# Turning attention probabilities on VectorE and through DRAM, in a streaming encoder layer

## The chip, the cores and the metric

One core of one Trainium2 chip runs the program. The metric is the time of one execution on the device in microseconds. TensorE (PE) multiplies matrices and writes PSUM; VectorE (DVE) and ScalarE (ACT) do the element-wise work; GpSimd (POOL) only clears memory at the start. SyncE (SP) issues the loads of weights; ACT issues all other transfers except part of the first loads and last stores. All numbers are float32. A product in near float32 accuracy is made of `fp32r` operands: a value is split into a high part (a rounded copy) and a low part (the rest), and high x high, high x low and low x high are added up.

## The reference

One layer on 256 prompt tokens and 64 sample tokens, 320 together, model width 2048:

```
xn = rmsnorm(x)
h  = xn @ w_in                      # columns [u | v | q | k | v_attn]
u, v = gelu(h[u]), gelu(h[v])       # gMLP branch, 2048 wide each
q, k = rope(h[q]), rope(h[k])       # 32 query heads, 4 key heads, 64 wide
a  = u * (masked ws @ layernorm(v) + bs)      # mixing inside chunks of 128 tokens
s  = q k^T / 8, by chunks of 64 queries       # keys: this chunk and the two before it
p  = exp(s - m) / (sum exp(s - m) + exp(sink - m))
o  = p @ v_attn
x += (sigmoid(g_a) * (a @ w_branch_a) + sigmoid(g_b) * (o @ w_branch_b)) @ w_out
x += swiglu(rmsnorm(x));  y = rmsnorm(x)
```

The outputs are y for both token sets, the new keys and values, and the normalised v of the sample.

## The kernel before

Activations stay in SBUF with features on partitions and the 320 tokens along the row, split into a high and a low part (`xh`, `xl`). Weights are streamed. `gemm` (line 136) makes 512 output columns: for each block of 256 contraction rows it takes a weight block, already split into `hi` and `lo`, and issues 24 matmuls with 320 columns. `fetch` (119) loads raw blocks of 512 KB on SP, four buffers deep; `prepare` (128) splits a block two blocks ahead, `hi` on ACT (L107) and `lo` on DVE (L110), three buffers deep. If either is late, PE waits. The order of products is in `products` (49): first k and v_attn (`kv`), then the four q and four v products in the order of `QV`, then the gate of the attention branch (`mm_gb`), its branch product (`mm_bb`), u, the other gate, the other branch, w_out and the feed-forward part.

All other work is put between the matmuls by a calendar. `later(slots, fn)` (90) books a function some slots ahead; `pump` (96) runs after every twelve matmuls and issues what is due. So a `gemm` of 16 contraction chunks has 16 slots. After the `kv` product the framework may also reorder instructions when it schedules.

The attention works on a group of 8 query heads with one key head at a time (`g` of 4). `q_done` (515) copies a q product out of PSUM, swaps the rope halves with four small transfers issued by ACT (`rope_swap`, 329), turns them on DVE (`rope_turn`), splits the queries into high and low (`q_parts`, 421), and books five steps, five slots apart, beginning `QK0[g]` slots after the product. A step `n` takes 64 queries of 8 heads as 4 tiles of 128 rows, against 64, 128 or 192 keys (`NK`); its keys' values are in one or two blocks of 64 or 128 keys (`VB`). It has four functions (`attend`, 441):

- `scores`, slot 0: 8 matmuls into two PSUM banks; maximum on DVE; exponential on ACT, which also adds up the denominator, into `pr`.
- `weigh`, slot 2: multiplies `pr` by the reciprocal denominator, two tiles on ACT and two on DVE.
- `turn`, slot 4: turns `pr` by TensorE, four transposes per key block into the PSUM tile `pt` (L486), and splits it into `ph` and `pl` (both called `p` for a block of 64 keys, whose other 64 partitions are zero).
- `values`, slot 6: for each key block two matmuls, value block `vv` with `ph` and with `pl` (L501). A value block holds the high parts in columns 0 to 63 and the low parts in 64 to 127, so partitions 0 to 63 of the result `o` are from the high values and 64 to 127 from the low ones. ACT copies the lower half out (L503), DVE adds both into `f1` (L509).

The blocks of new values are made by `new_v` (395): two transposes of v_attn per block (L398), a scale by the rms factor (`rv`, one column per block), a split. Five blocks are made; two groups of tokens are transposed twice, as blocks start at tokens 0, 64, 128, 192 and 256.

`v_done` (538) takes a v product: scale, gelu, transposes back to tokens (L547), statistics. Behind the attention come, from the calendar, the split of `f1` (`split_o`, 578) and the layer norm of v (`v_load` 589, `v_norm` 596).

Of the kernel before, what the change touches and what calls it, by code (L numbers as in the profile page):

```python
# [18 lines left out]
P = 128  # L19
# [14 lines left out]
    [(0, 4), (512, 4), (1024, 4), (1536, 4)],  # L34
    [(0, 4), (512, 4), (1024, 4), (1536, 2), (1792, 2)],
]
QV = [("q", 0), ("v", 0), ("q", 1), ("q", 2), ("v", 1), ("q", 3), ("v", 2), ("v", 3)]
QK0 = [14, 14, 24, 18]

NK = [64, 128, 192, 192, 192]  # L40
KC = [0, 0, 0, 64, 256]
VB = [[(0, 64)], [(0, 128)], [(0, 128), (2, 64)], [(1, 128), (3, 64)], [(4, 128), (5, 64)]]


def f32(ap):
    return ap.bitcast(F32)
# [23 lines left out]
def tile_hybrid_step(ctx: ExitStack, tc: tile.TileContext, a: dict, outs: list):  # L70
# [158 lines left out]
    rv = main.tile([P, 6], F32, name="rv")  # L229

    def x_norm():
        ssum = main.tile([P, 3], F32, name="ssum")
# [14 lines left out]
    def put_rope():  # L247
        nc.vector.tensor_tensor(cos_t, cos_t, rx, op=ALU.mult)
        nc.vector.tensor_tensor(sin_t, sin_t, rx, op=ALU.mult)
        for blk, i, p0, q0, n in (  # L250
            (0, 0, 0, 0, P), (1, 0, 64, 0, 64), (1, 1, 0, 64, 64), (2, 1, 0, 0, P), (3, 1, 64, 0, 64), (5, 2, 0, 0, 64)
        ):
            nc.vector.tensor_copy(rv[q0 : q0 + n, blk : blk + 1], rs1[p0 : p0 + n, i : i + 1])

    xt_d = dram.tile([P, DC, T], F32, name="xt_d")
    xst = {}
# [85 lines left out]

    ka = ap.tile([P, 4, NPOS], F32R, name="ka")
    kl = ap.tile([P, 4, NPOS], F32R, name="kl")
    vv = ap.tile([P, 6, 4, P], F32R, name="vv")
    vat = qr[:, 2:4, :]
    p64 = ap.tile([P, 2, 512], F32R, name="p64")
    nc.gpsimd.memset(f32(p64[64:P]), 0.0)
    for blk in (3, 5):
        nc.gpsimd.memset(f32(vv[64:P, blk]), 0.0)  # L350
    ck = ap.tile([P, 2, P], F32, name="ck")

    def split_v(blk, n, src):
        split(vv[:n, blk, :, 0:64], vv[:n, blk, :, 64:128], src.rearrange("p (g d) -> p g d", g=4))

    def rope_scale():
        nc.vector.tensor_scalar_mul(cos_t, cos_t, 0.125)
# [30 lines left out]
    def cached():  # L388
        pc = bank("pc")
        for t in range(2):  # L390
            nc.tensor.transpose(pc[:, t * P : (t + 1) * P], ckv[:, 0, t * P : (t + 1) * P], ident)
        nc.vector.tensor_copy(ck, pc[:, 0:256].rearrange("p (t k) -> p t k", t=2))
        split_v(4, P, ckv[:, 1, :])

    def new_v(blk, t0, n):
        pv = bank(f"pv_{blk}")
        for t in range(2):
            nc.tensor.transpose(pv[:n, t * P : (t + 1) * P], vat[:, t, t0 : t0 + n], ident)  # L398
        v = tmp.tile([P, 256], F32, tag="e1", name=f"vn_{blk}", bufs=4)[:n]
        nc.vector.tensor_scalar_mul(v, pv[:n, 0:256], rv[:n, blk : blk + 1])  # L400
        split_v(blk, n, v)
        if blk in (2, 5):
            dst = vo_p if blk == 2 else vo_s
# [37 lines left out]
    def attend(g, n, qs, st):  # L441
        nk, kc = NK[n], KC[n]

        def scores():
            sp = [bank(f"s_{g}_{n}_{i}") for i in range(2)]
            mx = ap.tile([P, 4], F32, tag="mx", name=f"mx_{g}_{n}", bufs=2)
            for j in range(4):
                o = sp[j // 2][:, (j % 2) * 256 : (j % 2) * 256 + nk]
                q2 = qs[:, j * 5 + n, :, :].rearrange("p e q -> p (e q)")
                nc.tensor.matmul(o, q2, ka[:, g, kc : kc + nk], start=True, stop=False)  # L450
                nc.tensor.matmul(o, q2, kl[:, g, kc : kc + nk], start=False, stop=True)
            for i in range(2):
                v = sp[i].rearrange("p (j k) -> p j k", j=2)[:, :, 0:nk]
                nc.vector.reduce_max(mx[:, 2 * i : 2 * i + 2], v, axis=AX.X)
            nm = ap.tile([P, 4], F32, tag="nm", name=f"nm_{g}_{n}", bufs=2)
            nc.vector.scalar_tensor_tensor(nm, mx, -1.0, nsink[:, 4 * g : 4 * g + 4], ALU.mult, ALU.min)
            es = ap.tile([P, 4], F32, tag="es", name=f"es_{g}_{n}", bufs=2)
            nc.vector.tensor_tensor(es, sink[:, 4 * g : 4 * g + 4], nm, op=ALU.add)
            nc.scalar.activation(es, es, AF.Exp)
            pr = ap.tile([P, 4, 192], F32, tag="pr", name=f"pr_{g}_{n}", bufs=2)  # L460
            den = ap.tile([P, 4], F32, tag="den", name=f"den_{g}_{n}", bufs=2)
            for j in range(4):
                o = sp[j // 2][:, (j % 2) * 256 : (j % 2) * 256 + nk]
                nc.scalar.activation(
                    pr[:, j, 0:nk], o, AF.Exp, bias=nm[:, j : j + 1], accum_out=den[:, j : j + 1]
                )
            st.update(pr=pr, den=den, es=es)

        def weigh():
            den, pr = st["den"], st["pr"]  # L470
            nc.vector.tensor_tensor(den, den, st["es"], op=ALU.add)
            nc.vector.reciprocal(den, den)
            for j in range(4):
                p = pr[:, j, 0:nk]
                if j % 2:
                    nc.vector.tensor_scalar_mul(p, p, den[:, j : j + 1])
                else:
                    nc.scalar.activation(p, p, AF.Copy, scale=den[:, j : j + 1])

        def turn():  # L480
            k0 = 0
            mm = []
            for bi, (blk, kn) in enumerate(VB[n]):
                pt = bank(f"pt_{g}_{n}_{bi}")
                for j in range(4):
                    nc.tensor.transpose(pt[:kn, j * P : (j + 1) * P], st["pr"][:, j, k0 : k0 + kn], ident)  # L486
                k0 += kn
                if kn == P:
                    ph = ap.tile([P, 512], F32R, tag="ph", name=f"ph_{g}_{n}")
                    pl = ap.tile([P, 512], F32R, tag="pl", name=f"pl_{g}_{n}")  # L490
                else:
                    ph, pl = p64[:, 0, :], p64[:, 1, :]
                split(ph[:kn], pl[:kn], pt[:kn])
                mm += [(vv[:, blk, g, :], ph), (vv[:, blk, g, :], pl)]
            st["mm"] = mm

        def values():
            po = bank(f"o_{g}_{n}")
            mm = st["mm"]
            for i, (l, r) in enumerate(mm):  # L500
                nc.tensor.matmul(po, l, r, start=(i == 0), stop=(i == len(mm) - 1))  # L501
            ol = tmp.tile([64, 512], F32, tag="st", name=f"ol_{g}_{n}")
            nc.scalar.activation(ol, po[64:128], AF.Copy)  # L503
            pov = po.rearrange("p (j e q) -> p j e q", j=4, e=2)
            olv = ol.rearrange("p (j e q) -> p j e q", j=4, e=2)
            oc = slice(4 * g, 4 * g + 4)
            tq = slice(n * 64, (n + 1) * 64)
            for e in range(2):
                nc.vector.tensor_tensor(  # L509
                    f1[64 * e : 64 * e + 64, oc, tq], pov[0:64, :, e, :], olv[:, :, e, :], op=ALU.add  # L510
                )

        return scores, weigh, turn, values

    def q_done(g, ps):
        for t in range(4):
            nc.scalar.activation(qr[:, t, :], ps[t], AF.Copy)
        qs = ap.tile([P, 20, 2, 64], F32R, tag="qs", name=f"qs_{g}")
        hi, lo = q_parts(g, qs)
        later(1, lambda: rope_swap(4))  # L520
        later(5, lambda: rope_turn(0))
        later(7, lambda: rope_turn(2))
        at = QK0[g]
        later(at - 5, lambda: hi(0))
        later(at - 4, lambda: lo(0))
        later(at - 3, lambda: hi(1))
        later(at - 2, lambda: lo(1))
        for n in range(5):
            scores, weigh, turn, values = attend(g, n, qs, {})
            later(at + 5 * n, scores)  # L530
            later(at + 5 * n + 2, weigh)
            later(at + 5 * n + 4, turn)
            later(at + 5 * n + 6, values)


    bst = main.tile([P, 3, 4, 6], F32, name="bst")
# [82 lines left out]
    at = 16  # L619
# [8 lines left out]
    later(at + 46, lambda: nc.scalar.dma_start(gv_s[0, 0], tok[0:64, 2, :]))  # L628
    later(at + 39, load_ws)
    later(at + 42, lambda: turn_ws(0))  # L630
    later(at + 43, lambda: turn_ws(1))

    def sigmoid(dst, ps, b0, g):
        for t in range(4):
# [247 lines left out]
```

## Time and profile before

| | |
|---|---|
| median of 3 runs | 1971.21 us (1970.22 to 1971.97) |
| the profiled execution | 1970.76 us |
| its span in the trace | 1968.9 us |
| PE / DVE / ACT busy | 99% / 52% / 42% of the span |
| first `mm_q` to first `mm_gb` | from 47 to 322 us |
| first scores, last values | 103 us, 353 us |

Busy time of PE counts overlapping matmuls once; their ends are modelled, so a busy PE says only that it was not waiting. Instructions that issue a transfer are not counted as busy; they show in rows marked ACTq and SPq. In rows of groups the columns are line, engine, operation, output and inputs, shapes and count, then busy time, the mean of one in ns, and the idle time in front of them with what ended it. In rows of the chain and of the timeline they are start, duration, what. A row of waits gives who waited for whom, the sum, how often, the longest. A row of windows gives the stretch and its length, then each engine's busy time and number of instructions, the clock granted to TensorE, the share of the DMA engines, and GB/s.

### The profile page before, as it was taken

The numbers are of one execution on the slowest core, as the hardware profiler recorded it, in microseconds if no ns is written. First come the engines' busy times: TensorE is split into PE (matmuls) and PEld (weight loads), VectorE is DVE, ScalarE is ACT, GpSimd is POOL, SyncE is SP. The second block draws the span as 40 slices with busy tenths as digits, with TensorE's granted clock in tenths as the row PEclk, the third lists the DMA queues.
The fourth block names the chain that finished last, engine by engine and source line by source line (L and its number), as shares of the span: only waits on it lengthen the run. The fifth ranks groups of instructions, "written<-read, shape, count | busy, mean of one in ns | idle before, by whom it ended". The sixth has DMA issues, their size and how long they took to land.

```text
span 1968.9 us, 31812 instructions
## 1 busy us (share of the span) xinstructions
PE 1948.7 (99%) x13327; PEld 1940.0 (99%) x13327; DVE 1028.6 (52%) x1513; ACT 817.1 (42%) x1219; POOL 5.6 (0%) x11
## 2 busy tenths in 40 slices
PE   9999999999999999999999999999999999999997
PEld 8999999999999999999999999999999999999996
DVE  5767777853445543454455444443444444444454
ACT  5575766633333443333343333333333333333343
POOL 1000000000000000000000000000000000000000
PEclk9999999999999999999999999999999999999998
DMA  8544433654444454445455555445555544555433
GB/s 266 157 121 133 118 112 118 181 184 150 150 140 139 140 150 150 150 150 204 150 150 149 147 152 151 150 147 151 149 149 148 153 151 149 147 151 150 152 130 102
DMA packets 152304, 294.82 MB, mean 150 GB/s; under 512 B 9521, under 2 KB 14593, under 8 KB 151969
## 3 DMA queue, kind: packets, MB, share of 16 engines
q1 hardware_dynamic: 147104, 281.05, 46.8%
q10 hardware_dynamic: 5056, 11.74, 1.9%
q8 instruction: 104, 1.70, 0.3%
q14 instruction: 40, 0.32, 0.0%
HBM read 285.86 MB, written 6.16 MB: 148 GB/s over the span
## 4 chain that ended last, share of the span: by engine, by line
PE 95%; ACT 1%; DVE 1%; DMA 1%; issue 0%; ACTq 0%; DVEq 0%; SPq 0%
PE mm_fu L152 5%; PE mm_fg L152 5%; PE mm_fd L152 5%; PE mm_fu L151 5%; PE mm_fg L151 5%; PE mm_fd L151 5%; PE mm_fd L153 5%; PE mm_fg L153 5%; PE mm_fu L153 5%; PE mm_u L151 2%; PE mm_ga L153 2%; PE mm_bb L153 2%; PE mm_wo L153 2%; PE mm_ba L153 2%; PE mm_bb L151 2%; PE mm_wo L152 2%
## 5 line engine op out<-in xcount | busy, mean ns | idle before, releaser
L110 DVE TENSOR_TENSOR lo<-raw,hi 128x1024 fp32r<-128x1024 f32 (+1 forms) x534 | 646.4, 1211 | 672.0 <-ACT hi L107 670.6
L107 ACT ACTIVATE hi<-raw 128x1024 fp32r<-128x1024 f32 (+1 forms) x533 | 559.4, 1050 | 1022.5 <-PE mm_fu L152 188.8
L151 PE MATMUL mm_fd<-xh,hi 128*128 128x320 f32 x704 | 218.5, 310 | 0.0
L151 PE MATMUL mm_fg<-yh,hi 128*128 128x320 f32 x704 | 217.8, 309 | 0.0
L151 PE MATMUL mm_fu<-yh,hi 128*128 128x320 f32 x704 | 217.5, 309 | 0.0
L152 PE MATMUL mm_fu<-yl,hi 128*128 128x320 f32 x704 | 217.5, 309 | 0.0
L153 PE MATMUL mm_fu<-yh,lo 128*128 128x320 f32 x704 | 217.5, 309 | 0.0
L153 PE MATMUL mm_fg<-yh,lo 128*128 128x320 f32 x704 | 217.5, 309 | 0.0
L152 PE MATMUL mm_fg<-yl,hi 128*128 128x320 f32 x704 | 217.5, 309 | 0.0
L152 PE MATMUL mm_fd<-xl,hi 128*128 128x320 f32 x704 | 217.4, 309 | 0.0
L153 PE MATMUL mm_fd<-xh,lo 128*128 128x320 f32 x704 | 217.4, 309 | 0.0
L152 PEld LDWEIGHTS mm_fd<-xl,hi 128*128 128x128 f32 x704 | 132.4, 188 | 0.0
L151 PEld LDWEIGHTS mm_fd<-xh,hi 128*128 128x128 f32 x704 | 132.4, 188 | 0.0
L153 PEld LDWEIGHTS mm_fd<-xh,lo 128*128 128x128 f32 x704 | 132.4, 188 | 0.0
L151 PEld LDWEIGHTS mm_fg<-yh,hi 128*128 128x128 f32 x704 | 132.2, 188 | 0.1
L152 PEld LDWEIGHTS mm_fg<-yl,hi 128*128 128x128 f32 x704 | 132.1, 188 | 0.1
L153 PEld LDWEIGHTS mm_fg<-yh,lo 128*128 128x128 f32 x704 | 132.1, 188 | 0.0
L151 PEld LDWEIGHTS mm_fu<-yh,hi 128*128 128x128 f32 x704 | 132.1, 188 | 0.0
L152 PEld LDWEIGHTS mm_fu<-yl,hi 128*128 128x128 f32 x704 | 132.1, 188 | 0.0
L153 PEld LDWEIGHTS mm_fu<-yh,lo 128*128 128x128 f32 x704 | 132.1, 188 | 0.0
L151 PE MATMUL mm_q<-xh,hi 128*128 128x320 f32 x256 | 81.4, 318 | 0.0
L151 PE MATMUL mm_v<-xh,hi 128*128 128x320 f32 x256 | 80.4, 314 | 0.0
(257 smaller groups left out, 3960.2 us busy)
## 6 DMA issues: line engine op xcount, KB each, us to landing
raw<-in_w_in_dram SPq DMA_DIRECT2D x104, 512.0 KB, 3.7
raw<-in_w_ffn_gate_dram SPq DMA_DIRECT2D x88, 512.0 KB, 3.7
raw<-in_w_ffn_up_dram SPq DMA_DIRECT2D x88, 512.0 KB, 3.6
raw<-in_w_ffn_down_dram SPq DMA_DIRECT2D x82, 512.0 KB, 3.6
raw<-in_w_gate_dram SPq DMA_DIRECT2D x64, 512.0 KB, 4.0
raw<-in_w_branch_b_dram SPq DMA_DIRECT2D x32, 512.0 KB, 3.6
raw<-in_w_branch_a_dram SPq DMA_DIRECT2D x32, 512.0 KB, 3.6
raw<-in_w_out_dram SPq DMA_DIRECT2D x32, 512.0 KB, 3.6
```

The source lines that it names most:

```text
L107: nc.scalar.activation(hi, src, AF.Copy)
L110: nc.vector.tensor_tensor(lo, src, f32(hi), op=ALU.subtract)
L151: nc.tensor.matmul(o, hi[:, c, cols], xh[:, k, :], start=(k == 0), stop=False)
L152: nc.tensor.matmul(o, hi[:, c, cols], xl[:, k, :], start=False, stop=False)
L153: nc.tensor.matmul(o, lo[:, c, cols], xh[:, k, :], start=False, stop=(k == nk - 1))
```

## The change

The step of the attention has six functions instead of four, at slots 0, 2, 3, 6, 8 and 10. `turn` is gone. `pack` transposes `pr` on DVE in blocks of 32x32 into `u`, and four transfers on ACT's queue write it to a DRAM scratch, in runs of 512 bytes, each from 32 partitions. `gather` reads it back with one transfer per key block (128 or 64 rows of 2 KB) into `pf`, on ACT's queue. `part` splits `pf`. For a block of 64 keys the high parts go to partitions 0 to 63 and the low parts to 64 to 127 of one tile `p2`, and the value block holds the high values twice, so one matmul takes the place of two. The order of the query rows inside a tile is another, which `values` undoes when it adds into `f1`.

Values are transposed once per 128 tokens (three times in place of five), and the overlapping blocks are copied. `pr` has one buffer in place of two; `pf` takes one from the tag `st`. The products q and v come in another order, the attention of a group starts at other slots, and the layer norm of v has steps of 9 slots in place of 10.

```diff
-QV = [("q", 0), ("v", 0), ("q", 1), ("q", 2), ("v", 1), ("q", 3), ("v", 2), ("v", 3)]
-QK0 = [14, 14, 24, 18]
+QV = [("q", 0), ("q", 1), ("v", 0), ("q", 2), ("v", 1), ("q", 3), ("v", 2), ("v", 3)]
+QK0 = [14, 24, 18, 13]
...
-VB = [[(0, 64)], [(0, 128)], [(0, 128), (2, 64)], [(1, 128), (3, 64)], [(4, 128), (5, 64)]]
+VB = [[(6, 64)], [(0, 128)], [(0, 128), (2, 64)], [(1, 128), (3, 64)], [(4, 128), (5, 64)]]
...
+    def split_v64(blk, src, b):
+
+        for h in (0, 64):
+            nc.scalar.activation(vv[h : h + 64, blk, :, 0:64], heads(src), AF.Copy)
+        nc.vector.tensor_tensor(
+            vv[0:64, blk, :, 64:128], heads(src), f32(vv[b : b + 64, blk, :, 0:64]), op=ALU.subtract
+        )
...
+    def v_blocks(i):
+        v = vn[i]
+        if i == 0:
+            split_v(0, v)
+            split_v64(6, v[0:64], 0)
+            nc.vector.tensor_copy(vv[0:64, 1], f32(vv[64:128, 0]))
+        elif i == 1:
+            split_v64(2, v[0:64], 0)
+            split_v64(3, v[64:128], 64)
+            nc.scalar.activation(vv[64:128, 1, :, 0:64], heads(v[0:64]), AF.Copy)
+            nc.vector.tensor_copy(vv[64:128, 1, :, 64:128], f32(vv[0:64, 2, :, 64:128]))
+        else:
+            split_v64(5, v, 0)
...
-    for i, (blk, t0, n) in enumerate([(0, 0, P), (1, 64, P), (2, 128, P), (3, 192, 64), (5, 256, 64)]):
-        later(6 + i, lambda blk=blk, t0=t0, n=n: new_v(blk, t0, n))
+    for i, n in xs:
+        later(6 + i, lambda i=i, n=n: new_v(i, i * P, n))
+        later(8 + 2 * i, lambda i=i: v_blocks(i))
...
-            pr = ap.tile([P, 4, 192], F32, tag="pr", name=f"pr_{g}_{n}", bufs=2)
+            pr = ap.tile([P, 4, 192], F32, tag="pr", name=f"pr_{g}_{n}")
...
-        def turn():
+        nb = nk // 32
+
+        def pack():
+            u = ap.tile([P, 6, P], F32, tag="u", name=f"u_{g}_{n}")
+            nc.vector.transpose(
+                u[:, 0:nb].rearrange("p k (j r) -> p j k r", j=4),
+                st["pr"][:, :, 0:nk].rearrange("p j (k c) -> p j k c", c=32),
+            )
+            d = st["d"] = dram.tile([6, 32, 4, P], F32, tag="pd", name=f"pd_{g}_{n}", bufs=3)
+            for b in range(4):
+                nc.scalar.dma_start(
+                    d[0:nb, :, b, :].rearrange("k c x -> c k x"), u[32 * b : 32 * b + 32, 0:nb, :]
+                )
+
+        def gather():
+            rows = st["d"].rearrange("k c b x -> (k c) (b x)")
+            pf = st["pf"] = tmp.tile([P, 2, 512], F32, tag="st", name=f"pf_{g}_{n}")
             k0 = 0
+            for i, (blk, kn) in enumerate(VB[n]):
+                nc.scalar.dma_start(pf[:kn, i, :], rows[k0 : k0 + kn, :])
+                k0 += kn
+
+        def part():
             mm = []
-            for bi, (blk, kn) in enumerate(VB[n]):
-                pt = bank(f"pt_{g}_{n}_{bi}")
-                for j in range(4):
-                    nc.tensor.transpose(pt[:kn, j * P : (j + 1) * P], st["pr"][:, j, k0 : k0 + kn], ident)
-                k0 += kn
+            for i, (blk, kn) in enumerate(VB[n]):
+                src = st["pf"][:kn, i, :]
+                l = vv[:, blk, g, :]
                 if kn == P:
                     ph = ap.tile([P, 512], F32R, tag="ph", name=f"ph_{g}_{n}")
                     pl = ap.tile([P, 512], F32R, tag="pl", name=f"pl_{g}_{n}")
+                    split(ph, pl, src)
+                    mm += [(l, ph), (l, pl)]
                 else:
-                    ph, pl = p64[:, 0, :], p64[:, 1, :]
-                split(ph[:kn], pl[:kn], pt[:kn])
-                mm += [(vv[:, blk, g, :], ph), (vv[:, blk, g, :], pl)]
+                    p2 = ap.tile([P, 512], F32R, tag="p2", name=f"p2_{g}_{n}")
+                    split(p2[0:64], p2[64:128], src)
+                    mm += [(l, p2)]
             st["mm"] = mm
...
-        return scores, weigh, turn, values
+        return ((0, scores), (2, weigh), (3, pack), (6, gather), (8, part), (10, values))
...
-        later(at + 3 + 10 * g, lambda g=g: v_load(g))
+        later(at + 3 + 9 * g, lambda g=g: v_load(g))
         for i, n in xs:
-            later(at + 6 + 10 * g + 3 * i, lambda g=g, i=i, n=n: v_norm(g, i, n))
+            later(at + 6 + 9 * g + 3 * i, lambda g=g, i=i, n=n: v_norm(g, i, n))
```

More of the change, by code (lines that the diff above doesn't have):

```diff
@@ L249, in put_rope @@
         nc.vector.tensor_tensor(sin_t, sin_t, rx, op=ALU.mult)
[L250 to L253, printed above, removed]
     xt_d = dram.tile([P, DC, T], F32, name="xt_d")
@@ L344, in tile_hybrid_step, with heads, split_v @@
     kl = ap.tile([P, 4, NPOS], F32R, name="kl")
-    vv = ap.tile([P, 6, 4, P], F32R, name="vv")
+    vv = ap.tile([P, 7, 4, P], F32R, name="vv")
     vat = qr[:, 2:4, :]
[L347 to L350, printed above, removed]
+    for blk in (2, 3, 5, 6):
+        nc.gpsimd.memset(f32(vv[64:P, blk, :, 64:128]), 0.0)
     ck = ap.tile([P, 2, P], F32, name="ck")
-    def split_v(blk, n, src):
-        split(vv[:n, blk, :, 0:64], vv[:n, blk, :, 64:128], src.rearrange("p (g d) -> p g d", g=4))
+    def heads(src):
+        return src.rearrange("p (g d) -> p g d", g=4)
+    def split_v(blk, src):
+        split(vv[:, blk, :, 0:64], vv[:, blk, :, 64:128], heads(src))
+    def split_v64(blk, src, b):
[4 more added lines that the diff above has]
+        )
     def rope_scale():
@@ L528, in q_done @@
         for n in range(5):
[L529 to L533, printed above, removed]
+            for dt, step in attend(g, n, qs, {}):
+                later(at + 5 * n + dt, step)
     bst = main.tile([P, 3, 4, 6], F32, name="bst")
@@ L624, in tile_hybrid_step @@
     for g in range(4):
-        later(at + 3 + 10 * g, lambda g=g: v_load(g))
+        later(at + 3 + 9 * g, lambda g=g: v_load(g))
         for i, n in xs:
-            later(at + 6 + 10 * g + 3 * i, lambda g=g, i=i, n=n: v_norm(g, i, n))
[L628 to L631, printed above, removed]
+            later(at + 6 + 9 * g + 3 * i, lambda g=g, i=i, n=n: v_norm(g, i, n))
+    later(at + 43, lambda: nc.scalar.dma_start(gv_s[0, 0], tok[0:64, 2, :]))
+    later(at + 36, load_ws)
+    later(at + 40, lambda: turn_ws(0))
+    later(at + 41, lambda: turn_ws(1))
     def sigmoid(dst, ps, b0, g):
```

24 lines of the change are left out of this document (12 added, 12 removed).

## The prediction

> **What bounds the kernel now.** I read the page from the top: busy times, then the chain of work that ended last.
>
> ```profile
> span 1968.9 us, 31812 instructions
> PE 1948.7 (99%) x13327; PEld 1940.0 (99%) x13327; DVE 1028.6 (52%) x1513; ACT 817.1 (42%) x1219; POOL 5.6 (0%) x11
> ...
> PE 95%; ACT 1%; DVE 1%; DMA 1%; issue 0%; ACTq 0%; DVEq 0%; SPq 0%
> ```
>
> TensorE (PE) is 95% of the chain, so every microsecond of PE issue that is removed comes off the end, as long as nothing else makes PE wait. VectorE (DVE) and ScalarE (ACT) look half idle, but that is an average over the span. The change lies in one stage, so I asked for that stretch (the attention runs from 106 to 346 us), for the long rest, and for the stretch behind the attention.
>
> ```profile
> core 0: us, PE busy (x) PEld busy (x) DVE busy (x) ACT busy (x) POOL busy (x), PEclk, DMA share, GB/s
> 106.00:346.00 240.00, 238.51 (x1665) 234.00 (x1664) 175.07 (x344) 162.37 (x385) 0.00 (x0) 1.00 0.41 119
> 300.00:1900.00 1600.00, 1599.67 (x10943) 1598.50 (x10942) 779.43 (x1030) 596.28 (x750) 0.00 (x0) 1.00 0.50 152
> 360.00:420.00 60.00, 60.00 (x411) 60.00 (x410) 48.27 (x78) 27.11 (x34) 0.00 (x0) 1.00 0.72 209
> ```
>
> In the attention DVE is at 175/240 = 73% and ACT at 162/240 = 68%, and PE is idle for 1.5 us in all. The clock granted is 1.00, so less PE work buys no faster clock. From the second row a matmul starts every 1600/10943 = 0.146 us; one slot of the calendar is twelve, 1.76 us, and attention work comes on top of it.
>
> **What PE loses.** The chain shows what the removed operations cost in issue time.
>
> ```profile
> 123.18 0.44 PE pt L486 x4
> 128.02 0.47 PE o L501 x2
> 133.77 0.88 PE pt L486 x8
> 139.06 0.92 PE o L501 x4
> 145.26 0.87 PE pt L486 x8
> ...
> 59.05 0.22 PE pv L398 x2
> ```
>
> - Transposes of the probabilities: a group of heads has two steps with one key block (0.44 us) and three with two (0.88 us), 3.52 us; four groups, 14.1 us. All 128 go.
> - Value products: each of the 16 blocks of 64 keys needs one matmul in place of two, 48 in place of 64 in all. One costs 0.92/4 = 0.23 us; 16 are 3.7 us.
> - Transposes of new values: three blocks of tokens in place of five, 2 x 0.22 = 0.4 us.
>
> All of it lies on PE, which sets the end: 18.2 us. The reordered q and v products are the same 1,536 matmuls, so PE pays nothing for the order. Attention still runs nearly without a break (starts at slots 30, 56, 82 and 109 after the kv product, before at 30, 62, 88 and 114), so its added work is spread much as before; the one tight place is the fourth group, which starts 13 slots after its product where none before had under 14; if its queries come a slot late, that is 2 us, once.
>
> **What DVE gains.** Each of the 20 steps gets one 32x32-block transpose of 4 x 64, 4 x 128 or 4 x 192 elements per partition: 12,288 in all. No row shows this operation. Bounds come from the slopes of these:
>
> ```profile
> L110 DVE TENSOR_TENSOR lo<-raw,hi 128x1024 fp32r<-128x1024 f32 x72 | 87.8, 1220 | 30.7 <-ACT hi L107 29.9
> L110 DVE TENSOR_TENSOR pl<-pt,ph 128x512 fp32r<-128x512 f32 x16 | 11.0, 686 | 3.7 <-ACT ph L107 3.4
> L476 DVE TENSOR_SCALAR pr<-pr,den 128x192 f32<-128x192 f32 x24 | 7.0, 318 | 0.4
> L476 DVE TENSOR_SCALAR pr<-pr,den 128x64 f32<-128x64 f32 x8 | 1.7, 251 | 0.1
> ```
>
> The first pair gives (1220-686)/512 = 1.04 ns per element and 0.15 us to start; the second 0.52 ns and 0.22 us. So 20 transposes are 11 to 16 us, the largest 0.6 to 0.95 us. I take the upper end, since a transpose has to pass every element. DVE then has 175 + 16 = 191 us in a stretch of 240 - 17 = 223 us: 86%. It cannot be a gain, as no DVE work of size goes. The splits keep their sizes; they only read SBUF where they read PSUM. The copied value blocks are five more short ACT operations and six fewer on DVE, before the attention starts, where PE has no use for them yet: nothing.
>
> **What ACT gains.** All new transfers are issued by ACT: four per step to DRAM (80), and one or two back (32). An issue occupies ACT's sequencer, which page and windows do not count as busy.
>
> ```profile
> L331 ACTq DMA_DIRECT2D swp<-qr x10: 632/632/1226, 47.0 to 252.5; - x10
> ...
> L385 ACTq DMA_DIRECT2D out_dram<-kout x1: 345/345/345, 66.3 to 66.3; - x1
> L386 ACTq DMA_DIRECT2D out_dram<-kout x1: 565/565/565, 66.8 to 66.8; - x1
> ```
>
> Transfers of 128 partitions took 0.35 us, of 64 partitions 0.57, of 8 partitions 0.63. The new ones have 32 partitions going out: 0.35 to 0.63 us each, 28 to 50 us; coming back 128 and 64 partitions: 11 to 18 us. In all 39 to 69 us; I take 0.5 us each, 56 us. Part of it is covered by the ACT instruction that is still running:
>
> ```profile
> 47.02 1.23 ACTq L331 DMA_DIRECT2D swp<-qr  x1
> 47.27 1.05 ACT L107 ACTIVATE hi<-raw 128x1024 fp32r<-128x1024 f32 x1
> 48.29 0.64 ACTq L332 DMA_DIRECT2D swp<-qr  x1
> 48.97 0.63 ACTq L331 DMA_DIRECT2D swp<-qr  x1
> 49.64 0.63 ACTq L332 DMA_DIRECT2D swp<-qr  x1
> 50.32 1.06 ACT L107 ACTIVATE hi<-raw 128x1024 fp32r<-128x1024 f32 x1 [2.00 <-PE mm_q L152]
> ```
>
> One burst of four stood in front of ACT for at most 2.0 us (the row names PE as what ended it), and 1.3 of its 3.3 us ran under a split. With that share (40%), 34 of my 56 us are exposed: ACT has 162 + 34 = 196 us in 223, 88%. So ACT and DVE have room left, but little, and both are on the way of every weight block (`hi` on ACT, `lo` on DVE). What stands behind a waiting issue on ACT is the next `hi`. PE is two blocks (2 x 24 x 0.146 = 7 us) behind the split that ACT makes, and ACT is often early:
>
> ```profile
> ACT hi L107 <- PE mm_v L152: 14.6, 8, 2.5
> ACT hi L107 <- PE mm_q L152: 11.1, 9, 2.5
> ```
>
> Here ACT waited for PE to free a buffer, up to 2.5 us at a time; a wait of that length costs nothing.
>
> **Does the longer route arrive in time?** Scores to value products was 6 slots; now it is 10. These rows follow one step of 192 keys.
>
> ```profile
> 125.21 0.25 PE L450 MATMUL s<-ka,qs 128*128 128x192 f32 x1
> ...
> 131.34 0.79 ACT L478 ACTIVATE pr<-pr,den 128x192 f32<-128x192 f32 x2
> ...
> 132.35 0.32 DVE L476 TENSOR_SCALAR pr<-pr,den 128x192 f32<-128x192 f32 x1
> ```
>
> The weighted probabilities are ready 7.5 us after the scores began. Steps followed each other after 145.26 - 133.77 = 11.5 us; without 0.88 us of transposes and 0.23 us of products they follow after 10.4 us, 2.08 us per slot. Then: transposed at 8.5; four issues; the last begins at 9.5 to 10.4. For the landing I have
>
> ```profile
> raw<-in_w_ffn_down_dram SPq DMA_DIRECT2D x12, 256.0 KB, 2.7
> xt_d<-st ACTq DMA_DIRECT2D x4, 640.0 KB, 3.3
> out_dram<-tok ACTq DMA_DIRECT2D x3, 512.0 KB, 3.7
> ```
>
> so the pieces of at most 96 KB should be down after 2.7 us at most, at 12.2 to 13.1. The way back is issued in slot 6, at 12.5: a wait of 0.6 us at worst. It brings 384 KB, 3.2 us between the rows for 256 and 512, and its second issue starts 0.5 us later: 16.2 to 16.8, against the splits in slot 8 at 16.6. They take some 2 to 2.5 us (two copies on ACT and two subtractions on DVE, none above the 0.69 us of the `pl` row, overlapping), to about 19.1, against the value products in slot 10 at 20.8. The slack is 1.7 us, 0.5 if one more pair of weight splits gets ahead. DMA has room: 6.3 MB go each way in this stretch, and the row 360:420 shows PE without a gap at a DMA share of 0.72, where the attention has 0.41.
>
> **The sum.** PE gives 18.2 us. PE stood 1.5 us in this stretch with 32% of ACT idle; with 12% idle I take it as 32/12 times as much, 4.0 us, so 2.5 us are lost; the bounds are 0 (less pressure on PSUM could even give the 1.5 us back) and the rivals below. Net 15.7 us. The profiled execution took 1970.8 us (span 1968.9), so 1955.1 us; the median of the three runs is 0.4 us above it: 1955.5. My own range for this case is 1951 to 1960.
>
> **Rivals.** *Part of the gain goes in waits for landings.* If writes take 1 us longer than I took and the loads behind them too, the slack turns into a PE wait of 0.3 to 0.5 us in each of 20 steps, 6 to 10 us: 1961 to 1966. For it: the probabilities now make two trips through DMA, the rows above have no 32-partition write, and the slack is small. Against: the `out_dram` write landed no later than weight loads of its size (3.7 us). The Trainium skill ("DMA: Bandwidth & Descriptors", section "Anatomy of one DMA — SWDGE (gpsimd) path") says that most of a transfer's fixed 2 us is the receipt of the last write, and that it can be surprisingly long when HBM is the target. The `xt_d` and `out_dram` rows do not show such a delay.
>
> *All of the gain goes.* A PE wait of 0.9 us per step, half a slot, eats 18 us: 1967 to 1975. It needs the chain to be 2.6 us later than worked out.
>
> *Slower: ACT becomes the bound.* If nothing covers the issues and each costs 0.63 us, ACT has 162 + 69 = 231 us for 223. ACT also has to stand in order for the transpose, for the landing of the way out and for that of the way back. This decides as soon as those waits pass (240 - 231)/20 = 0.45 us per step; at 1 us each step ACT has 251 us, 11 us above the 240 us of before: 1982. For it: ACT's idle time was 78 us, and up to 69 are claimed. Against: the burst above ran 40% covered, and early `hi` splits absorb waits of 2.5 us. The Trainium skill ("VectorE: DVE Perf Modes", section "Rules for kernel authors") points the same way: a full 128x128 turn belongs on TensorE where PSUM may hold the result, and the DVE's own is for 32x32 blocks. That rule prices the operation alone; the 95% of the chain above says which engine's time counts here.
>
> **Chances.** Forecast 0.52, part of the gain 0.18, gain eaten 0.10, slower by ACT 0.20. A measurement of this kernel tells about 0.2%, 4 us, from no change. The third case is mostly within it, so: faster 0.70, same 0.09, slower 0.21. The range reaches from the forecast's low end through the partial cases to a little above no change, 1951 to 1973; left out is the ACT rival.
>
> **What would show it.** Right: no `pt` group, 48 `o` matmuls, PE still at 99%, the stretch from the first `mm_q` to the first `mm_gb` shorter by 15 to 18 us, ACT and DVE near 88% in it, the transposes 16 us in sum, issues near 0.5 us. Each term is wrong if its row differs. The forecast is wrong if PE's idle time in the attention passes 10 us: with `o` waiting on the splits it is the landings, with `mm` waiting on `hi` or `lo` it is ACT.

## The result and the profile after

The changed kernel takes 1984.79 us (median of 4 runs, 1982.87 to 1985.93) against 1971.02 for the kernel before on the same chip. The ratio is 1.0069, with a 95% interval of 1.0051 to 1.0086: slower by 13.8 us, where I had forecast 15.7 us faster. All executions of these two kernels agree within 0.2%, so the 0.7% is clear of the noise.

The head of its page:

```profile
span 1983.7 us, 31744 instructions
PE 1942.1 (98%) x13179; PEld 1926.8 (97%) x13179; DVE 1043.6 (53%) x1527; ACT 820.4 (41%) x1224; POOL 4.7 (0%) x12
...
PE 82%; DMA 1%; DVE 1%; ACT 1%; issue 0%; ACTq 0%; DVEq 0%
```

PE has 148 matmuls fewer (128 transposes, 16 value products, 4 transposes of values) and a longer span. Two stretches hold all of the difference: the q and v products with the attention, and the gate product behind them. First the kernel before (columns as in the rows of windows above), then the changed one:

```profile
47.00:322.00 275.00, 273.84 (x1907) 269.41 (x1906) 203.09 (x393) 178.90 (x398) 0.00 (x0) 1.00 0.44 128
322.00:443.00 121.00, 120.67 (x829) 119.86 (x829) 87.60 (x150) 62.55 (x106) 0.00 (x0) 1.00 0.57 170
```

```profile
47.00:332.00 285.00, 268.69 (x1785) 258.63 (x1784) 216.78 (x413) 182.25 (x410) 0.00 (x0) 0.99 0.57 161
332.00:458.00 126.00, 121.43 (x803) 119.44 (x803) 88.77 (x144) 62.42 (x97) 0.00 (x0) 0.97 0.59 179
```

The first is 10 us longer, the second 5. PE stood (275 - 273.84) + (121 - 120.67) = 1.5 us in the two before, and 16.3 + 4.6 = 20.9 us after. ACT is not at its limit by this row: 182 us of 285, and some 50 us of issues that the row leaves out. The sizes that I had to estimate came out close:

```profile
L504 DVE STREAM_TRANSPOSE u<-pr 128x768 f32<-128x768 f32 x12 | 11.7, 975 | 2.8 <-ACT pr L498 2.7
L504 DVE STREAM_TRANSPOSE u<-pr 128x512 f32<-128x512 f32 x4 | 2.8, 708 | 0.1
L504 DVE STREAM_TRANSPOSE u<-pr 128x256 f32<-128x256 f32 x4 | 1.8, 443 | 0.5 <-ACT pr L498 0.4
...
L510 ACTq DMA_DIRECT2D pd<-u x80: 309/460/562, 109.1 to 350.5; - x80
L519 ACTq DMA_DIRECT2D pf<-pd x32: 338/415/515, 114.5 to 354.0; - x32
```

The transposes are 11.7 + 2.8 + 1.8 = 16.3 us (16 forecast), the issues 80 x 0.46 + 32 x 0.42 = 50 us (56 forecast). So the sizes of the added work are not what failed. PE's own waits between 47 and 375 us name what did:

```profile
PE o L542 <- DVE pl L110: 2.9, 6, 1.0
PE o L542 <- ACT ph L107: 2.8, 4, 0.8
PE o L542 <- DVE p L110: 2.8, 2, 1.8
PE mm_q L153 <- DVE lo L110: 2.7, 3, 1.0
PE s L470 <- DVE qs L457: 2.7, 2, 2.2
PE mm_v L153 <- DVE lo L110: 1.5, 1, 1.5
PE mm_q L151 <- ACT hi L107: 1.3, 2, 0.8
```

Half of it (8.5 us) is value products that wait for the split probabilities: the chain comes late. A third (5.5 us) is weights, `hi` and `lo`, and the rest is queries. One stretch of ACT's timeline shows how the queue makes both late. The scores of this step began at 248.4 us.

```profile
254.69 0.34 ACTq L519 DMA_DIRECT2D pf<-pd  x1
255.13 0.80 ACT L498 ACTIVATE pr<-pr,den 128x192 f32<-128x192 f32 x2 [2.00 <-DMA pd<-u]
...
257.41 1.82 ACTq L510 DMA_DIRECT2D pd<-u  x4
259.28 1.09 ACT L559 ACTIVATE qr<-mm_q 128x320 f32<-128x320 f32 x3 [1.30 <-DMA pd<-u]
...
264.18 0.63 ACTq L327 DMA_DIRECT2D swp<-qr  x1
264.94 0.92 ACTq L519 DMA_DIRECT2D pf<-pd  x2
266.19 1.06 ACT L107 ACTIVATE hi<-raw 128x1024 fp32r<-128x1024 f32 x1 [2.42 <-PE mm_v L153]
...
269.45 0.63 ACT L107 ACTIVATE ph<-pf 128x512 fp32r<-128x512 f32 x1 [1.50 <-DMA pf<-pd]
```

At 255.1 the weighting of this step had stood 2.0 us behind the way back of the step before, which waited for the landing of its way out. This step's way out was issued by 259.2, and by the completion marks in the trace all of it had landed only at 263.2, 4.4 us after its last issue began. Its way back was issued at 264.9, since other work, with a rope swap, was ahead of it in ACT's order. By my plan it was due in slot 6, 12.5 us after the scores, at 260.9. So of the 4.0 us that it was late, about half is the landing and half the order. The split began at 269.5, 21 us after the scores, when the product should have started. Between 47 and 375 us five waits of ACT, 12.1 us in all, ended with the landing of a way out.

The clock adds to it. These rows are from the changed kernel, before and behind two of the longest waits:

```profile
289.00:294.00 5.00, 3.53 (x23) 3.09 (x21) 3.21 (x6) 2.90 (x4) 0.00 (x0) 1.00 0.48 152
294.00:299.00 5.00, 4.28 (x18) 3.58 (x18) 4.89 (x10) 2.05 (x11) 0.00 (x0) 0.66 0.20 41
...
400.00:405.00 5.00, 2.59 (x18) 2.33 (x16) 3.73 (x7) 3.22 (x4) 0.00 (x0) 0.98 0.41 136
405.00:410.00 5.00, 4.14 (x15) 4.14 (x16) 5.00 (x7) 0.00 (x0) 0.00 (x0) 0.50 0.57 181
410.00:420.00 10.00, 10.00 (x65) 10.00 (x64) 6.70 (x10) 3.18 (x3) 0.00 (x0) 0.92 0.73 198
```

Behind three of PE's waits the granted clock falls to half: 0.34 x 5 = 1.7 us lost at 294, and 0.1 + 2.5 + 0.8 = 3.4 us at 400 to 420. A third place (225 to 235 us, clock 0.83) costs 1.7. Together 6.8 us, a part of it inside the waits themselves; the kernel before has no such place between 20 and 1950 us.

The rows of waits and of the clock can't simply be added up, but the starts of the matmuls in the two traces close the sum, from the first `mm_q` to the first `mm_bb`. I compare the time from one start to the next with what the same two kinds of matmul take without a wait. PE had 30 waits. They took 26.1 us by the starts (20.9 us in their rows, so each is some 0.17 us longer than its row), against 2.0 us before. The matmuls at half clock took 5.8 us longer. By the same starts PE did not give up 18.2 us but about 16.3: the transposes of the probabilities held the next matmuls up by 12.3 us in all, where I had read 14.1 from durations in the chain. So 24.1 us of waits and 5.8 us of clock stand against 16.3 + 13.8 = 30.1 us.

### The profile page after: what moved, and what is told of

It reads as the page before. It is cut to its first block, busy times and chain, and to the rows that moved or that the text cites. A ratio compares the mean times of both kernels' runs of the same rounds, so it can differ in the third digit from the quotient of the medians.

```text
span 1983.7 us, 31744 instructions
## 1 busy us (share of the span) xinstructions
PE 1942.1 (98%) x13179; PEld 1926.8 (97%) x13179; DVE 1043.6 (53%) x1527; ACT 820.4 (41%) x1224; POOL 4.7 (0%) x12
## 4 chain that ended last, share of the span: by engine, by line
PE 82%; DMA 1%; DVE 1%; ACT 1%; issue 0%; ACTq 0%; DVEq 0%
PE mm_fd L153 5%; PE mm_fu L151 5%; PE mm_fd L151 5%; PE mm_fg L151 5%; PE mm_fg L153 5%; PE mm_fu L153 5%; PE mm_fu L152 5%; PE mm_fg L152 5%; PE mm_fd L152 5%; PE mm_u L151 2%; PE mm_ba L153 2%; PE mm_ba L152 2%; PE mm_bb L152 2%; PE mm_bb L151 2%; PE mm_wo L152 2%; PE mm_ga L152 2%
## 5 line engine op out<-in xcount | busy, mean ns | idle before, releaser
L153 PE MATMUL mm_gb<-xh,lo 128*128 128x320 f32 x256 | 78.8, 314 | 3.6 <-DVE lo L110 3.6
```

Source lines behind the costliest of these rows:

```text
L153: nc.tensor.matmul(o, lo[:, c, cols], xh[:, k, :], start=False, stop=(k == nk - 1))
```

## The experiments

Theory A: ACT's queue, in order, stands for issues, transposes and landings, and what is behind comes late. Theory B: the chain with two landings is longer than its 10 slots. Theory C: the steps of 9 slots of the norm make the wait in the gate product. Ratios are against the kernel before on the same chip, and 0.001 is 2 us. What a run costs over the kernel before is taken from its ratio; what it saves against the changed kernel is the difference of the two medians.

**The norm steps alone** (`e1_space10`).

```diff
-        later(at + 3 + 9 * g, lambda g=g: v_load(g))
+        later(at + 3 + 10 * g, lambda g=g: v_load(g))
```

and the steps that follow, as before the change.

> The changed kernel with the layer norm of v at steps of 10 slots again, as before the change. Theory C (the steps of 9 put the load of the next gains in front of ACT while it must wait for the last norm, PE then stands 3.6 us at 402 us, and the clock granted falls to 0.5 for two windows): the gate stage (first mm_gb to first mm_bb) falls from 126.6 us to about 120, the time by 5 to 6 us, to 1979. Rival (the gate stage is late only because ACT comes late out of the attention): the stage stays within 1.5 us, 1985.

1983.21 us, ratio 1.0060 (1.0044 to 1.0076). The gate product took 126.9 us, and PE's longest wait in it was 3.8 us. Theory C falls.

**Who issues** (`e2_sp`, `e2_pool`).

```diff
-                nc.scalar.dma_start(
+                nc.sync.dma_start(
                     d[0:nb, :, b, :].rearrange("k c x -> c k x"), u[32 * b : 32 * b + 32, 0:nb, :]
...
-                nc.scalar.dma_start(pf[:kn, i, :], rows[k0 : k0 + kn, :])
+                nc.sync.dma_start(pf[:kn, i, :], rows[k0 : k0 + kn, :])
```

(`nc.gpsimd` in the second.)

> The changed kernel with all 112 scratch transfers issued by SP in place of ACT. Theory A (ACT's queue, in order, stands for issues and landings, and weight splits and copies behind it come late): first mm_q to first mm_gb falls from 285 us to 272 or less, PE waits in it fall by more than half, time 1972 or less. Theory B (the chain through two landings is longer than its 10 slots, whoever issues): the waits of the value products on the splits stay, time within 4 us of the changed kernel, 1981 to 1989. If SP's own waits for weight buffers hold the transfers up, PE waits of the value products grow and it is slower than 1985.

> The same with the transfers issued by GpSimd, which has nothing else to do in this stretch. Theory A: as for SP, 272 us or less in the stretch and 1972 or less. Theory B: unchanged within 4 us, or slower by what GpSimd's issue takes longer.

SP: 1972.81 us, ratio 1.0011 (1.0002 to 1.0021), 12 us less. PE's waits between 47 and 375 us with SP:

```profile
PE o L542 <- ACT ph L107: 7.9, 6, 3.6
PE o L542 <- DVE pl L110: 2.2, 6, 0.6
PE o L542 <- DVE p L110: 1.6, 2, 1.1
PE mm_v L153 <- DVE lo L110: 0.3, 1, 0.3
```

and its two stretches:

```profile
47.00:323.00 276.00, 265.30 (x1785) 257.56 (x1785) 216.29 (x412) 181.57 (x414) 0.00 (x0) 0.99 0.59 168
323.00:444.00 121.00, 119.07 (x808) 117.32 (x806) 89.27 (x146) 60.67 (x96) 0.00 (x0) 1.00 0.60 183
```

Weights and queries come in time now, and the long wait in the gate product is gone. The value chain is later still: 11.7 us of waits where there were 8.5. This is A and B side by side. The first stretch fell to 276 us, not to the 272 expected, and PE's waits in these rows from 16.7 to 12.0 us, not by half: there theory A's forecast missed. The wait for weights went as it said, and its time was missed by 0.8 us. Theory B's 1981 to 1989 us missed too. The gate product took 121 us with steps of 9, which again is against C. GpSimd: 1991.28 us, ratio 1.0102 (1.0086 to 1.0118). PE's wait of `o` for `ph` is 16.3 us there: off ACT, but the chain is later still (the products began 23.5 us after the scores, median). The clock was at half in five places from 130 us on. Theory A's forecast for this run missed.

**Which half** (`e6_gather_sp`: only `pf` on SP; `e7_pack_sp`: only `d` on SP).

> Only the way back (32 transfers) on SP; the 80 to DRAM stay on ACT, slots 6, 8, 10. Splits theory A: if it is ACT's standing for the landing of the way out that costs (4.0 us from last issue to first way back, in order on ACT), most of the 12 us that SP brought come with this part: 1973 to 1976. If it is the issue time (80 of 0.46 us remain, 37 of 50 us), most of the loss stays: 1980 to 1984.

> The other half: the 80 transfers to DRAM on SP, the 32 back on ACT. Issue time: ACT loses 37 of 50 us of issues, 1973 to 1977. Standing for landings: ACT still waits for the way out in order, 1980 or more.

1978.12 us (1.0037, 1.0024 to 1.0051) and 1974.37 us (1.0016, 1.0006 to 1.0026). The first lies between its two forecasts, the second in the one for issue time. Neither half has it all, 6.7 and 10.4 us of SP's 12.0. It does not tell issuing from standing, as the way out also stands for the transpose.

**A longer chain** (`e3_late`, `e5_sp_late`).

```diff
-        return ((0, scores), (2, weigh), (3, pack), (6, gather), (8, part), (10, values))
+        return ((0, scores), (2, weigh), (3, pack), (7, gather), (10, part), (13, values))
...
-    at = 16
+    at = 18
```

In these two the split of chunks 2 and 3 of the attention's 16 comes after the gate has been written over them, so that part of the output is not the reference's; the instructions are the same.

> The changed kernel, transfers on ACT, with three more slots for the chain: gather at 7, part at 10, values at 13 in place of 6, 8 and 10 (what follows the attention starts 2 slots later). Theory B (half of the loss is the chain: in the changed kernel the products started 21.9 us after the scores, where 10 slots would be 20.8): PE's waits for ph, pl and p go, those for hi, lo and qs stay; time about 1973 to 1977. Theory A alone (all PE waits come from ACT's backlog, the chain being late because ACT is): ACT's work is the same, so the time stays within 4 us, 1981 to 1989.

> Both: transfers on SP and the three more slots. With SP alone (1972.8) PE waited only for the value chain, 10 to 12 us, and no longer for weights. If A and B together are the whole loss, no wait is left and the 18.2 us that PE gives up show: 1953 to 1956, faster than both kernels. If DVE is the next bound (it has 86% to do in this stretch), lo comes late and it stays at 1960 or above.

On ACT 1976.79 us (1.0031, 1.0018 to 1.0044): 8 us less, theory B's number. But its place is another. These are the two stretches of this run:

```profile
49.00:333.00 284.00, 268.94 (x1788) 259.05 (x1787) 215.04 (x411) 181.55 (x412) 0.00 (x0) 0.99 0.58 162
333.00:451.00 118.00, 118.00 (x805) 117.02 (x805) 89.65 (x146) 63.05 (x98) 0.00 (x0) 1.00 0.64 190
```

The gate product fell by 8 us, from 126 to 118: its long wait and the half clock behind it are gone, where what follows the attention starts 2 slots later. The first stretch fell by 1 us. In the rows between 47 and 375 us PE's waits for `ph`, `pl` and `p` fell from 8.5 to 2.3 us, as theory B said, but those for `lo` and `hi` rose from 5.5 to 8.3, and queries still came late. So the longer chain moved the waits, and that it is worth 8 us by itself is not shown. On SP 1969.80 us (0.9995, 0.9986 to 1.0005): 15 us less, level with the kernel before, and 14 to 17 us above the 1953 to 1956 expected. A and B are not all. The first stretch took 276 us, as with SP alone: the value chain's waits are gone, and others stand in their place, the longest 3.7 us for queries and 3.7 us for an exponential on ACT. None of them is for `lo`.

**The longest chain that fits** (`e10_sp_mid`: on SP, slots 6, 9, 12, `at` unchanged).

> The changed kernel with transfers on SP and gather, part and values at slots 6, 9 and 12, the most that fits before the late tiles open. Between the run with SP alone (1972.8) and the one with 7, 10, 13 (1969.8): about 1970, PE's waits for ph gone.

1971.76 us (1.0004, 0.9994 to 1.0013). The waits for `ph` fell to 1.2 us, but the wait in the gate product was back, 3.3 us at 387 us.

**The buffer in the gate product** (`e12_gb2`, and `e13_sp_mid_gb2` on top of e10).

```diff
-        gb = late["pool"].tile([P, 2, W], F32, tag="gb", name=f"gb_{g}", bufs=1)
+        gb = late["pool"].tile([P, 2, W], F32, tag="gb", name=f"gb_{g}", bufs=2)
```

In the changed kernel, ACT's timeline around the wait at 402 us, then DVE's (two rows of it) and PE's:

```profile
396.15 0.33 ACTq L631 DMA_DIRECT2D gb<-in_gmlp_ln_g_dram  x1
396.52 0.49 ACTq L632 DMA_DIRECT2D gb<-in_gmlp_ln_b_dram  x1
397.05 1.28 ACT L677 ACT_TABLE_LOAD   x1 [4.36 <-DVE tok L640]
398.34 1.92 ACT L677 ACTIVATE f<-f,vec 128x320 f32<-128x320 f32 x4
400.17 3.12 ACT L107 ACTIVATE hi<-raw 128x1024 fp32r<-128x1024 f32 x3
```

```profile
401.27 0.69 DVE L639 TENSOR_TENSOR tok<-tok,gb 128x512 f32<-128x512 f32 x1 [2.42 <-DMA gb<-in_gmlp_ln_g_dram]
404.60 2.35 DVE L110 TENSOR_TENSOR lo<-raw,hi 128x1024 fp32r<-128x1024 f32 x2
```

```profile
405.86 0.64 PE L153 MATMUL mm_gb<-xh,lo 128*128 128x320 f32 x1 [3.27 <-DVE lo L110]
```

The load of the next gains has one buffer, so its issue stands on ACT until DVE's last norm is done (L640), and three `hi` splits come in one go behind it. DVE in turn stands 2.4 us for the landing of that load and then does six operations of the norm, and only then comes `lo`.

> The changed kernel with two buffers for the gains and offsets of the layer norm (gb), so that ACT's load of the next pair no longer waits for DVE's last norm, nor DVE for the load just behind it. If the stand of PE at 402 us (3.6 us, and two windows at half clock behind it) is this single buffer, which the new order of work now meets at a bad time, the gate stage falls from 126.6 to about 121 us: 1979 to 1981. Rival (the gate stage is late from the attention's backlog): within 2 us of 1984.8.

> Transfers on SP, slots 6, 9, 12, and two buffers for gb: without the stand of 3.6 us at 387 us in the gate stage and the half clock behind it, 1966 to 1967 instead of 1971.8. What is left above 1953 is then the starts of the groups (4.0 us at 148, 3.0 us at 215, the clock, 1.5 us at 286) and small waits. If the stand moves elsewhere, 1970 or more.

e12: 1981.20 us (1.0045, 1.0031 to 1.0059), and this row for its gate product:

```profile
336.00:456.00 120.00, 119.11 (x808) 117.63 (x807) 89.06 (x144) 62.96 (x99) 0.00 (x0) 1.00 0.62 188
```

120 us at full clock in place of 126: with the second buffer the wait is gone. The one buffer needs the bad moment too, since the wait was also gone with SP (121 us) and with the later start (118 us). The medians differ by only 3.6 us; in the profiled execution, the slowest of the five, the q products began 3 us later than in the changed kernel's and the first stretch was 1 us longer. e13: 1969.92 us, ratio 0.9988 (0.9979 to 0.9997): now just faster than the kernel before, and 3 us above what I expected. In its trace two other places, at the starts of groups, fell to half clock for 6.8 us each.

**The order alone** (`e8_order`: the kernel before with the new `QV` and `QK0`).

> The kernel before with only the order of the q and v products and the start slots of the changed one; probabilities on TensorE, values at slot 6. My prediction: the order costs nothing, 1971 within 3 us. Rival (the starts of a group, with its query splits, now meet the gelu of a v product, and that is where PE still stands for 4 us at a time when transfers are on SP and the chain is long): 1975 or more, with PE waiting for qs or for PSUM banks.

1974.05 us (1.0014, 1.0004 to 1.0023). The order costs 2.8 us without any of the rest. PE had no long wait at a group's start; it stood 1.9 us for `lo` at 394 us, in the gate product, with half clock behind it. DVE had stood 2.8 us for the load of the gains just before, so by this trace the new order makes the single buffer bite; two buffers were not tried in this run. The rival's place was wrong here, but not with the longer chain. This is e13's ACT and PE at the start of the second group:

```profile
147.29 2.55 ACT L449 ACTIVATE qs<-qr 64x1280 fp32r<-64x1280 f32 x2
149.86 1.28 ACT L479 ACT_TABLE_LOAD   x1
151.16 0.21 ACT L479 ACTIVATE es<-es 128x4 f32<-128x4 f32 x1
```

```profile
152.35 0.90 PE L586 MATMUL vt<-ident,v 128*128 128x128 f32 x3 [3.65 <-ACT pr L484]
```

Query splits and a table load (gelu of a v product lies just ahead) hold the exponentials up, and PE waits 3.7 us for a PSUM bank that they read.

**Less work on DVE** (`e11_lessdve`, on top of e10).

```diff
-                u[:, 0:nb].rearrange("p k (j r) -> p j k r", j=4),
-                st["pr"][:, :, 0:nk].rearrange("p j (k c) -> p j k c", c=32),
+                u[:, 0:1].rearrange("p k (j r) -> p j k r", j=4),
+                st["pr"][:, :, 0:32].rearrange("p j (k c) -> p j k c", c=32),
...
```

Here `u` is one tile that is cleared once, and the transfers go on SP at slots 6, 9 and 12 as in e10.

> As the run with slots 6, 9, 12 on SP, but each transpose on DVE turns one block of 32 keys instead of two to six (the rest of what is sent stays zero, so the attention's output is left incomplete): DVE's 16 us of transposes fall to about 6 and nothing else changes. If DVE is the bound that is left, 5 us or more come off against that run. If what is left is the place where query splits meet the v products, it stays within 3 us of it.

1968.37 us (0.9992, 0.9982 to 1.0001), 3.4 us less than e10 with overlapping intervals: between the two expectations. DVE's transposes take part; they are not the bound.

**The added work as dead weight** (`e9_issue`, `e14_dead_wait`, `e16_dead_sp`). The kernel before, with its transposes on TensorE, and in each step, called at slots 3 and 6:

```diff
+            for b in range(4):
+                nc.scalar.dma_start(
+                    d[0:nb, :, b, :].rearrange("k c x -> c k x"), u[32 * b : 32 * b + 32, 0:nb, :]
+                )
...
+                nc.scalar.dma_start(pf[:kn, i, :], rows[k0 : k0 + kn, :])
```

In e9 the source is `xh`, which is long there; in e14 it is DVE's transpose `u` of `pr`, which also has one buffer there, as in the changed kernel; e16 is e14 with `nc.sync`.

> The kernel before, whole, with the 112 scratch transfers added on ACT as dead weight: at slots 3 and 6 of each step, the same shapes, written from the split input and read back into a tile that nothing reads. ACT issues and stands for the landing of the way out; there is no wait for a transpose, and no work depends on the way back. Theory A in pure form: ACT's queue alone costs 8 us or more, 1979 or later, with PE waiting for hi, lo and pt. If ACT's backlog only hurts together with a tight chain, 1971 to 1974.

> The kernel before with the DVE transposes and all scratch transfers on ACT as dead weight, now with their true waits: ACT's issue has to stand for the transpose, which stands for the weighted probabilities, and the way back for the landing of the way out. Order, slots and TensorE's transposes are those of before (pr has one buffer). Nothing depends on what comes back. Issues alone cost nothing (1969.6). If standing in order behind these waits is ACT's cost, PE waits for hi, lo and pt appear and it is 1975 or more. If also this is free, the loss needs the tight chain: 1969 to 1972.

> The dead-weight kernel with true waits (DVE transposes and scratch transfers added to the kernel before, nothing depends on them; 1979.2 with the transfers on ACT), now with the transfers on SP. If its 8.5 us are ACT standing in order behind the transposes and landings, they go: 1970 to 1973. If they are the 16 us that DVE has more, they stay: 1977 or more.

e9: 1969.62 us (0.9992, 0.9982 to 1.0001), no cost. It says less than I wanted: with nothing to wait for, the framework moved the issues into ACT's idle time (31 of the 80 were issued before the first scores). So issue time that can lie anywhere cost nothing here. e14: 1979.23 us (1.0038, 1.0023 to 1.0053), 7.5 us for work on which nothing depends. This is ACT in it:

```profile
242.50 0.59 ACT L478 ACTIVATE pr<-pr,den 128x64 f32<-128x64 f32 x2
244.56 2.82 ACTq L490 DMA_DIRECT2D pd<-u  x4
247.43 0.59 ACT L107 ACTIVATE p<-pt 64x512 fp32r<-64x512 f32 x1 [4.34 <-issue]
```

The copy `p` stood 4.3 us behind four transfers that waited for a transpose and then took 2.8 us to issue. PE's product waited 1.4 us for it. In all PE waited 3.0 us for `pr` and 0.2 us for a weight block, so here the weights came in time. e16: 1975.80 us (1.0021, 1.0012 to 1.0031), 4.1 us over the kernel before. So of the 7.5 us about 3.4 go with ACT's queue (the intervals overlap, so that split is not sharp) and 4 stay with DVE's transposes, the single buffer of `pr` and the transfers.

**The stacked blocks alone** (`e4_stack`, and `e15_stack_gb2` with two buffers for gb): the kernel before with `split_v64`, `v_blocks` and this in `turn`:

```diff
+                    p2 = ap.tile([P, 512], F32R, tag="p2", name=f"p2_{g}_{n}")
+                    split(p2[0:64], p2[64:128], pt[:64])
+                    mm += [(vv[:, blk, g, :], p2)]
```

> The kernel before with only the stacked blocks of 64 keys and the three transposes of new values; the probabilities are still turned by TensorE, and order and slots are those of before. All theories: PE loses 16 value products and 4 transposes, 3.7 + 0.4 us; ACT and DVE get nothing in the attention. 1967 against 1971. If PE's share of the gain were wrong too, it would be 1970 or more.

> The best version so far (the kernel before with stacked 64-key blocks, 1967.7) with two buffers for gb. Its gate stage shows no stand of PE, so nothing should come off: 1967 to 1968.

1967.71 us, ratio 0.9984 (0.9974 to 0.9993), and 1968.22 us, 0.9984 (0.9974 to 0.9993). 3.2 us off, of 4.1 forecast: the part of the change that only takes work from PE pays, and it beats both kernels.

## Why the prediction was wrong, point by point

- **What PE gives up, 18.2 us.** The counts are as forecast. The 4.1 us of it that could be tried alone gave 3.2. The 14.1 us of transposes could not be taken away without the rest; by the starts of the matmuls in the trace of the kernel before they were 12.3, so the 18.2 should have been 16.3.
- **DVE 16 us, ACT's issues 56 us.** Right: 16.3 and 50.
- **The sum, "PE stood 1.5 us in this stretch with 32% of ACT idle; with 12% idle I take it as 32/12 times as much".** This is the step that failed. I had 2.5 us for it, and by the starts of the matmuls it was 24.1 us of waits and 5.8 us of clock. A share of idle time says nothing of waits when two engines that work in order wait for each other. Idle time comes in pieces that lie in the wrong place.
- **"What stands behind a waiting issue on ACT is the next `hi`", with two blocks of lead.** Only partly so. The weighting of the next step, the copies of the queries, the exponentials that free PSUM, and the chain's own `ph` stood there too, and none of them has a lead. Weights were a third of PE's named waits.
- **The chain, 19.1 us with 1.7 to spare.** Measured over the 20 steps, the products began 21.9 us (median) after the scores, where I had 20.8 for slot 10. The transposes began after 9.4 us rather than 7.5, as `weigh` queued behind other waits, and the way back was issued 4.4 us after the last way out began, where I had 2.1 to 3.0. The landing of the way out, put at 2.7 us at most, took 3.8 us (median of the steps, 1.6 to 5.4), so the rival of late landings was right about this term. In half of the steps the way back was issued at that landing, in the others up to 2.9 us behind it. The times of issue and split were right (1.8 and 2.5 us). A slack worked out from one quiet step was no slack.
- **The order "pays nothing".** True for PE's count. It cost 2.8 us by what it does to ACT and DVE. The one long wait in that run's trace was in the gate product, which my sum left out.
- **The clock.** I noted that less work buys no faster clock and overlooked that waits buy a slower one. The Trainium skill ("TensorE: Matmul & The Clock Gate", section "Part 1: The HAM clock gate (the "warmup" mystery)") says that the clock goes to half after an idle window of about 3.4 us. The trace has the half and the 3.4 us, but it came also behind waits of 2.2 us (292 us), so shorter waits than the page's rule count here. The third place follows waits of 0.5 and 0.8 us; most of the 30 waits had no half clock behind them.
- **The ACT rival, 1982 us at a chance of 0.20.** Its time was right within 3 us, which was in part luck, as its price was not: it had the issues as the larger part (69 us) and 1 us of standing per step. Movable issues were free, standing was not, and SP takes 12 us off. In the profiled executions the first stretch is 9 us shorter with SP and the gate product 6. Three more slots took 8 us off on ACT, nearly all in the gate product, and 3 us on SP; SP and the slots together take 15. So the value chain was late, but making it longer is not shown to pay for itself.
- **What stays open.** With transfers on SP, slots 6, 9, 12 and the second buffer, 2.4 us of PE's 16.3 are left. In that run's trace PE's waits took 12.0 us by the starts, against 2.0 before, and half clock 5.8. The longest are the group starts (3.7 and 2.6 us), with the clock behind them. e16 adds 4 us of work with the transposes, the single buffer of `pr` and the transfers. How much each takes was not separated.

## What to carry to other kernels

Before moving work from a busy engine to half-idle ones, list for each instruction that will wait what is behind it in its queue and how much lead the consumer of that has; a share of busy time gives no such answer. An issue that waits belongs on the queue where it holds up work with the longest lead (here SP, whose loads run four buffers ahead). Take the part that only removes work by itself: the stacked blocks alone beat both kernels.

## What the runs showed of the hardware that I had not expected

The granted clock fell to 0.50 for 3.4 or 6.8 us behind single waits of PE of 2.2 and 3.3 us and behind two of 0.5 and 0.8 us, which in the changed kernel cost 5.8 us beside the waits themselves. Transfers of at most 96 KB to DRAM from 32 partitions had all landed 3.8 us (median) after the last issue began. Transfers issued by GpSimd left the value products waiting for `ph` 16.3 us, against 7.9 from SP. A transfer from 32 partitions took 0.46 us to issue, and four that had to wait for their data held ACT for 4.3 us.
